# Key projection folded into the query projection, and expert indices from sixteen step positions

## The chip, the cores and the metric

The kernel runs on one core of a Trainium2 chip (TensorE, VectorE, ScalarE, POOL, and SyncE, which issues most transfers). The metric is the device time of one execution, in microseconds; the profile is of one further execution on the same kind of core.

## The reference

One encoder layer on 1024 tokens of width 1024, all in f32. A chunkwise mLSTM (4 heads of 256, chunks of 128 tokens, both directions) and an RG-LRU run side by side, are merged by sigmoid gates, and a product-key expert search follows. What the change touches:

```python
q = jnp.einsum("bshd,hde->bhse", xc, w_q)                  # xc = silu(conv(x))
k = jnp.einsum("bshd,hde->bhse", xc, w_k) / math.sqrt(d)   # q and k meet only as q . k
...
scores = jnp.einsum("thpc,hpnc->thpn", q, keys32)          # 8 heads, 2 halves, 128 keys
s_top, i_top = lax.top_k(scores, 16)
cand = s_top[:, :, 0, :, None] + s_top[:, :, 1, None, :]   # 16 x 16 sums
cand_idx = i_top[:, :, 0, :, None] * 128 + i_top[:, :, 1, None, :]
best, pos = lax.top_k(cand, 16)
idx = jnp.take_along_axis(cand_idx, pos, axis=-1)
gate = jax.nn.softmax(best, axis=-1)
act = gelu(expert_u[idx] . h)                              # 128 experts a token
out = sum_k (gate * act) * expert_v[idx]
```

The normalised scores are all that uses `k` in the mLSTM: within a chunk as q . k, between chunks through a state that sums k v and is read by q.

## The kernel before

Tiles have 128 partitions. Products that need precision are three products of rounded parts (`mm3`: high by high, high by low, low by high); others are plain f32 (`mm8`, `mm`).

Stages, in order. First the input projection with the LRU (to some 390 us). Then four mLSTM heads (some 400 to 920 us): `ml_x` projects and convolves a head's input, `ml_qkv` makes queries, keys and values, `ml_core` runs the chunks; merge-gate projections (`mg`) and output gates fill in. Working tiles come from one pool of 18 (`M1_BUFS`). `mixer_plan` lists the weights in order of use; an entry with an engine is split into high and low parts ahead of time, by ScalarE and POOL (`WENG`), an entry with None stays as loaded. Three raw weight buffers exist.

Then the branch merge in three groups of 2, 3 and 3 blocks of 128 tokens (L851, eight calls for each of 40 weight tiles a group), which ends in the scores of each block, kept in DRAM. Beside groups 1 and 2 runs `side`, a generator: for each of blocks 0 to 4 ("dense") `topk` finds the 16 best experts of each head and `gmat` turns indices and gates into a gate matrix over all 16384 experts; block 5 only gets `topk` (`prep`). The numbers that the generators yield are costs by which side work is laid beside the merge; the tile scheduler then fixes the order of each engine's queue ahead of the run.

`topk` takes the 16 best of 128 for the 16 half heads (`top16`), adds their scores along a staircase of 50 candidates that can be among the 16 best sums (`STAIR`: row a of the staircase has its own first position and length), and takes the 16 best of the 50 with their places. The indices of the winners come from a table `ci` of the 50 candidates' indices that POOL builds. For each head a one-hot matrix of 50 by 16 is made on VectorE (L1052), multiplied by the table on POOL (L1055) and reduced on VectorE (L1057). `gmat` splits each index by shift and mask (L1071 to L1075) into row and column, transposes them on TensorE and builds one-hot tiles (L1098, L1099, L1102; a quarter to a half of the L1102 products run on POOL).

The last stage (from some 1745 us) is the dense part: for each of 128 expert rows, products with all experts for five blocks (`ustep`, `vstep`), while the other three blocks fetch their own experts row by row (L1334, indirect transfers issued by POOL) into 8 row buffers, and VectorE multiplies and sums them (L1357, L1365). `topk` of blocks 6 and 7 is taken in steps between these, with the row buffers as its work tiles.

Of the kernel before, what the change touches and what calls it, by code (L numbers as in the profile page):

```python
# [8 lines left out]
F32 = mybir.dt.float32  # L9
F32R = mybir.dt.float32r  # L10
F16 = mybir.dt.float16
# [8 lines left out]
D = 1024  # L20
S = 1024
NB = 8
H = 4
# [11 lines left out]
class K:  # L35
# [13 lines left out]
    def x(self, dt=F32):  # L49
        return self.xp.tile([128, 1024], dt, name=self.name("x"), tag="x", bufs=self.x_bufs)  # L50
# [491 lines left out]
    def ml_x(self, h, done=None):  # L542

        nc = self.nc
        st = {}
        st["xm"], st["xc"] = [], []
        for e in range(2):
            blk = 2 * h + e
            x = self.pad_proj(blk, done if e == 0 else None)
            hi, lo = self.u(F32R), self.u(F32R)  # L550
            self.split(x[:, 2:2 + S], hi[:, :S], lo[:, :S])
            st["xm"].append((hi, lo))
            xc = self.u()
            self.conv(xc, x, V_MCW, V_MCB, blk)

            def act(xc=xc):
                nc.scalar.activation(xc[:, :S], xc[:, :S], AF.Silu)
                hi, lo = self.u(F32R), self.u(F32R)
                self.split(xc[:, :S], hi[:, :S], lo[:, :S])
                st["xc"].append((hi, lo))  # L560

            if e == 0:
                act()
            else:
                self.later = act
        return st

    def ml_qkv(self, h, st):
        nc = self.nc
        wh, wl = self.ws_get(("qk", h))  # L570
        for i, nm in enumerate(("q", "k")):
            st[nm] = []
            for e in range(2):
                t = self.u()
                for hf in range(2):
                    c = slice(hf * 512, hf * 512 + 512)
                    p = self.psg()
                    for cb in range(2):
                        o = i * 512 + cb * 256 + e * 128
                        self.mm3(p, (wh[:, o:o + 128], wl[:, o:o + 128]),  # L580
                                 (st["xc"][cb][0][:, c], st["xc"][cb][1][:, c]), cb == 0, cb == 1)
                    nc.scalar.activation(t[:, c], p, AF.Copy, scale=1.0 if i == 0 else 1.0 / 16.0)
                st[nm].append(t)
# [164 lines left out]
    def mixer_plan(self):  # L748
# [29 lines left out]
        for s_ in seq:  # L778
# [227 lines left out]
    def topk(self, b, res, x=None, keep=None):  # L1006
# [18 lines left out]
        ci = self.small([128, 8, self.NCAND], tag="ci", bufs=self.tb)  # L1025
        self.stair(nc.vector, cand, v)
        self.stair(nc.gpsimd, ci, ixf)
# [17 lines left out]
        idf = keep([128, 8, 16], tag="idf", bufs=2)  # L1045
        n = self.NCAND
        pr = [None] * 8
        for h in range(9):
            if h < 8:
                oh = self.small([128, n, 16], F16, tag="oh", bufs=2)  # L1050
                v8 = lambda z: z.rearrange("p a (u k) -> p a u k", k=8)
                nc.vector.tensor_tensor(v8(oh), self.iota_p[:, :, None, :].to_broadcast([128, n, 2, 8]),  # L1052
                                        v8(ph[:, h:h + 1].to_broadcast([128, n, 16])), op=OP.is_equal)
                pr[h] = x()[:, :n * 16].rearrange("p (a k) -> p a k", k=16)
                nc.gpsimd.tensor_tensor(pr[h], oh, ci[:, h][:, :, None].to_broadcast([128, n, 16]), op=OP.mult)  # L1055
            if h > 0:
                nc.vector.tensor_reduce(idf[:, h - 1], pr[h - 1].rearrange("p a k -> p k a"), axis=AX.X, op=OP.add)  # L1057
                pr[h - 1] = None
            if h % 2:
                yield 1.1  # L1060
        res["id"], res["gate"] = idf.rearrange("p h k -> p (h k)"), gate.rearrange("p h k -> p (h k)")
# [5 lines left out]
    def gmat(self, b, res):  # L1067

        nc = self.nc
        ii = self.x(I32)[:, 0:384].rearrange("p (a k) -> p a k", k=128)  # L1070
# [3 lines left out]
        ijf = self.x()[:, 0:256].rearrange("p (a k) -> p a k", k=128)  # L1074
        nc.vector.tensor_copy(ijf, ii[:, 1:3])  # L1075
        yield 1.0
# [232 lines left out]
    def prep(self, b, res, x=None):  # L1309
# [3 lines left out]
        self.nc.vector.tensor_copy(res["idi"], res["id"])  # L1313
        yield 0.1

    def gather(self, blocks):
        nc = self.nc
        KB = 8
        row = lambda: self.gkeep([128, D], tag="row", bufs=self.ROWS)
# [55 lines left out]
    def late_consts(self):  # L1375
        nc = self.nc
        A = self.A
        n = self.NCAND
        self.iota_p = self.cp.tile([128, n, 8], F16, name="iota_p")
        nc.gpsimd.iota(self.iota_p, pattern=[[1, n], [0, 8]], base=0, channel_multiplier=0, allow_small_or_imprecise_dtypes=True)  # L1380
# [171 lines left out]
def host(**i):  # L1552
# [10 lines left out]
    d["mwq"], d["mwk"], d["mwv"] = hw(a["mlstm_w_q"]), hw(a["mlstm_w_k"]), hw(a["mlstm_w_v"])  # L1563
# [30 lines left out]
```

## Time and profile before

| | |
|---|---|
| median of 3 runs | 3574.14 us (3561.7 to 3575.13) |
| profiled execution | 3566.02 us, span of its instructions 3563.9 us |
| TensorE / VectorE / ScalarE / POOL busy | 94% / 82% / 39% / 48% |

PE is TensorE's multiplying side and PEld its loading of weights, DVE is VectorE, ACT ScalarE. In a row of stretches the busy times stand in the order PE, PEld, DVE, ACT, POOL. A row of waits names the waiting engine, tile and line, and behind the arrow what it waited for. A group's last part is the idle time before its instructions. The share of the clock that TensorE was granted is 1.00 at its full 2.4 GHz.

### The profile page before, as it was taken

To read this page: it belongs to the slowest core of one execution; us is meant where nothing else is said; L and a number is where in the kernel's file an instruction comes from. 1 tells how busy PE (TensorE), PEld (TensorE's weight loads), DVE (VectorE), ACT (ScalarE), POOL (GpSimd) and SP (SyncE) were. 2 spreads that over 40 slices of the span, in tenths; PEclk is the share of its full clock that TensorE was granted. 3 is DMA by queue.
4 is the path that set the end of the run, shared out by engine and by line. 5 is a ranking of instruction groups with operands and counts; after the bars stand their busy time and mean duration, and the time that the engine had idled before them with its cause. 6 is when DMAs were issued, how large, how long until landed. Compare 5 with 4: busy or idle time off the path is not lost. (4 is left out here: it accounts for less than half of the span.)

```text
span 3563.9 us, 48538 instructions
## 1 busy us (share of the span) xinstructions
PE 3343.9 (94%) x17633; PEld 2827.0 (79%) x17633; DVE 2929.6 (82%) x5279; ACT 1392.0 (39%) x2565; POOL 1713.4 (48%) x1336
## 2 busy tenths in 40 slices
PE   7999999899899899878899999999999999999998
PEld 5787788778685565556788888998888999999987
DVE  8777574674327866998899999989999999999998
ACT  4565655655120240233333333343333334333333
POOL 7445354444102322342455555655555665666663
PEclk9999999999999999989899999999999999999999
DMA  2122211111466575558888879997887999999996
GB/s 107 60 71 68 72 51 51 63 48 44 154 217 208 159 251 199 174 170 258 312 318 301 283 275 342 360 338 276 314 284 279 341 357 351 344 347 334 352 348 239
DMA packets 319665, 812.56 MB, mean 228 GB/s; under 512 B 25600, under 2 KB 137408, under 8 KB 319424
## 3 DMA queue, kind: packets, MB, share of 16 engines
q0 software_dynamic: 115200, 419.48, 32.4%
q1 hardware_dynamic: 115184, 333.21, 26.7%
q10 hardware_dynamic: 89040, 56.76, 5.3%
q8 instruction: 138, 2.26, 0.3%
q14 instruction: 103, 0.84, 0.1%
HBM read 726.35 MB, written 83.00 MB: 227 GB/s over the span
## 5 line engine op out<-in xcount | busy, mean ns | idle before, releaser
L1334 POOL DMA_INDIRECT k<-in_pv,k x384 | 514.0, 1338 | 378.6 <-DVE k L1365 182.3
L1334 POOL DMA_INDIRECT k<-in_pu,k x384 | 506.6, 1319 | 332.7 <-DVE k L1357 148.0
L84 PE MATMUL ps<-h2h,wh 128*128 128x320 f32 x2048 | 637.2, 312 | 10.2 <-DVE u L1268 9.9
L85 PE MATMUL ps<-h2l,wh 128*128 128x320 f32 x2048 | 635.2, 310 | 0.0
L86 PE MATMUL ps<-h2h,wl 128*128 128x320 f32 x2048 | 628.9, 310 | 5.8 <-DVE wl L71 5.8
L851 PE MATMUL ps<-u,wr 128*128 128x384 f32 (+1 forms) x1920 | 581.1, 460 | 5.5 <-DMA u<-d 3.4
L1357 DVE SCALAR_TENSOR_TENSOR k<-k,rs,k 128x1024 f32<-128x1024 f32 x384 | 493.5, 1289 | 28.4 <-DMA k<-in_pu,k 28.4
L851 PEld LDWEIGHTS ps<-u,wr 128*128 128x128 f32 x1920 | 366.4, 194 | 181.7 <-issue 11.6
L85 PE MATMUL ps<-vl,wdh 128*128 128x512 f32 x1280 | 501.9, 393 | 2.5 <-DVE vl L71 2.5
L84 PE MATMUL ps<-vh,wdh 128*128 128x512 f32 x1280 | 469.0, 395 | 35.1 <-DVE u L1268 17.4
L1365 DVE SCALAR_TENSOR_TENSOR k<-k,k,k 128x1024 f32<-128x1024 f32 x384 | 494.6, 1288 | 0.4
L86 PE MATMUL ps<-vh,wdl 128*128 128x512 f32 x1280 | 494.3, 391 | 0.0
L84 PEld LDWEIGHTS ps<-h2h,wh 128*128 128x128 f32 x2048 | 388.1, 190 | 23.3 <-DVE u L1268 17.0
L86 PEld LDWEIGHTS ps<-h2h,wl 128*128 128x128 f32 x2048 | 385.6, 189 | 8.0 <-DVE wl L71 6.3
L85 PEld LDWEIGHTS ps<-h2l,wh 128*128 128x128 f32 x2048 | 387.8, 189 | 4.5
L1195 ACT ACTIVATE gel<-ps 128x320 f32<-128x320 f32 x256 | 111.1, 435 | 564.2 <-PE ps L86 549.4
L84 PEld LDWEIGHTS ps<-vh,wdh 128*128 128x128 f32 x1280 | 239.3, 189 | 88.2 <-DVE u L1268 22.5
L84 PE MATMUL ps<-h,wh 128*128 128x512 f32 x736 | 292.3, 399 | 14.0 <-ACT u L430 6.7
L86 PE MATMUL ps<-h,wl 128*128 128x512 f32 x736 | 290.8, 396 | 3.5 <-POOL wl L71 3.5
L85 PE MATMUL ps<-h,wh 128*128 128x512 f32 x736 | 291.0, 396 | 2.8 <-DVE h L253 2.8
L1238 ACT ACTIVATE gc<-gt 128x160 f32<-128x160 f32 x512 | 226.3, 510 | 155.9 <-DVE gel L1239 94.4
L86 PEld LDWEIGHTS ps<-vh,wdl 128*128 128x128 f32 x1280 | 241.4, 189 | 50.4
(327 smaller groups left out, 6079.1 us busy)
## 6 DMA issues: line engine op xcount, KB each, us to landing
wr<-in_u SPq DMA_DIRECT2D x128, 512.0 KB
wr<-in_v SPq DMA_DIRECT2D x128, 512.0 KB
d<-stg ACTq DMA_DIRECT2D x40, 1024.0 KB
gt<-d SPq DMA_DIRECT2D x64, 640.0 KB
wr<-in_win SPq DMA_DIRECT2D x49, 512.0 KB
wr<-in_wq SPq DMA_DIRECT2D x48, 512.0 KB
d<-u POOLq DMA_DIRECT2D x32, 512.0 KB
wr<-in_bm SPq DMA_DIRECT2D x24, 512.0 KB
```

The source lines that it names most:

```text
L84: mm(out, wh, mh, start=first, stop=False)
L85: mm(out, wh, ml, start=False, stop=False)
L86: self.lastmm = mm(out, wl, mh, start=False, stop=last)
L851: self.nc.tensor.matmul(p, w[:, cb * 128:cb * 128 + 128], m(cb), start=cb == 0, stop=cb == NB - 1)
L1195: nc.scalar.activation(gel[:, c], p, AF.Gelu)
L1238: nc.scalar.activation(gc[:, i * n:i * n + n], self.gt[j // 8, i][:, :, j % 8], AF.Copy)
L1334: nc.gpsimd.indirect_dma_start(out=t[:, :D], out_offset=None, in_=self.A["pu" if which == "u" else "pv"], in_offset=bass.IndirectOffsetOnA ...
L1357: nc.vector.scalar_tensor_tensor(r[:, :D], r[:, :D], self.rs2[:, b:b + 1], h2[:, :D], op0=OP.mult, op1=OP.mult, accum_out=dots[c][:, k % K ...
L1365: nc.vector.scalar_tensor_tensor(acc[:, :D], r[:, :D], ws[c][:, k % KB:k % KB + 1], acc[:, :D], op0=OP.mult, op1=OP.add)
```

## The change

The weights of queries and keys are handed over transposed and are no longer split. At the start of `ml_qkv` their product over the head's inner dimension is formed on TensorE in plain f32, scaled, and split in two parts; queries are projected with it, and the raw convolved input takes the keys' place in `ml_core`.

In `topk` the row of a winner in the staircase is the number of row starts that its place has reached. So its first index is the first of the list plus the sum of the steps between neighbours of the sorted list up to that row. Places of all 8 heads (128 numbers a token) are compared at once with 16 starts (`past`), multiplied by the steps (`steps`) and summed over 16 by halving (`total`). The start of the row is found in the same way and subtracted, and what is left selects the second index. All runs on VectorE, in 16-bit floats, over 16 x 128 elements. Row and column come out apart, so `gmat` takes them as they are; `prep` joins them again for the fetches.

```diff
@@ ml_x
+                st["k"].append(xc)
@@ ml_qkv
-        wh, wl = self.ws_get(("qk", h))
-        for i, nm in enumerate(("q", "k")):
...
+        raw = self.ws_get(("qk", h))
+        p = self.psg()
+        for cb in range(2):
+            for eb in range(2):
+                nc.tensor.matmul(p[:, cb * 256:cb * 256 + 256], raw[:, eb * 256 + cb * 128:eb * 256 + cb * 128 + 128],
+                                 raw[:, 512 + eb * 256:512 + eb * 256 + 256], start=eb == 0, stop=eb == 1)
+        t = self.u(F32R)
+        wh, wl = t[:, 0:512], t[:, 512:1024]
+        nc.scalar.activation(wh, p, AF.Copy, scale=1.0 / 16.0)
+        nc.vector.scalar_tensor_tensor(wl, p, 1.0 / 16.0, wh.bitcast(F32), op0=OP.mult, op1=OP.subtract)
+        st["q"] = []
...
@@ mixer_plan
-                plan.append((("qk", h), [(self.A["mwq"][h], 512), (self.A["mwk"][h], 512)], 1024, WENG))
+                plan.append((("qk", h), [(self.A["mwq"][h], 512), (self.A["mwk"][h], 512)], 1024, None))
@@ topk
-        ixf = self.small([128, 8, 2, 16], tag="tif", bufs=self.tb)
-        nc.vector.tensor_copy(ixf, ix)
-        nc.vector.tensor_scalar(ixf[:, :, 0], ixf[:, :, 0], 128.0, None, op0=OP.mult)
+        ixh = self.small([128, 2, 17, 8], F16, tag="ixh", bufs=self.tb)
+        nc.gpsimd.memset(ixh[:, :, 0], 0.0)
+        nc.vector.tensor_copy(ixh[:, :, 1:17], ix.rearrange("p h i a -> p i a h"))
+        dix = self.small([128, 2, 128, 2], F16, tag="dix", bufs=self.tb)
+        for i in range(2):
+            up, dn = (ixh[:, i, o:o + 16].rearrange("p a h -> p (a h)")[:, :, None].to_broadcast([128, 128, 2]) for o in (1, 0))
+            nc.vector.tensor_tensor(dix[:, i], up, dn, op=OP.subtract)
-        self.stair(nc.gpsimd, ci, ixf)
...
-        for h in range(9):
-            if h < 8:
-                oh = self.small([128, n, 16], F16, tag="oh", bufs=2)
...
-                nc.gpsimd.tensor_tensor(pr[h], oh, ci[:, h][:, :, None].to_broadcast([128, n, 16]), op=OP.mult)
-            if h > 0:
-                nc.vector.tensor_reduce(idf[:, h - 1], pr[h - 1].rearrange("p a k -> p k a"), axis=AX.X, op=OP.add)
...
+        def past(o, x, i):
+            nc.vector.tensor_tensor(octs(o), octs(x[:, None, :].to_broadcast([128, 16, 128])), tab(i), op=OP.is_ge)
+
+        def steps(o, m, i):
+            nc.vector.tensor_tensor(o.rearrange("p a (h u t) -> p (a h) u t", u=8, t=2),
+                                    m.rearrange("p a (h u t) -> p (a h) u t", u=8, t=2),
+                                    dix[:, i, :, None, :].to_broadcast([128, 128, 8, 2]), op=OP.mult)
+
+        def total(o, z):
+            for n in (8, 4, 2):
+                nc.vector.tensor_tensor(z[:, 0:n], z[:, 0:n], z[:, n:2 * n], op=OP.add)
+            nc.vector.tensor_tensor(o, z[:, 0], z[:, 1], op=OP.add)
+
+        m, z = wide(x(F16)), wide(x(F16))
+        past(m, pos, 0)
+        steps(z, m, 0)
+        total(ij[:, 0], z)
+        yield 3.6
+        nc.vector.tensor_tensor(octs(z), octs(m), tab(1), op=OP.mult)
+        rest = self.small([128, 2, 128], F16, tag="rest", bufs=self.tb)
+        total(rest[:, 0], z)
+        nc.vector.tensor_tensor(rest[:, 1], pos, rest[:, 0], op=OP.subtract)
+        yield 2.6
+        past(m, rest[:, 1], 2)
+        steps(z, m, 1)
+        total(ij[:, 1], z)
+        yield 3.6
@@ gmat
-        nc.vector.tensor_copy(ii[:, 0], res["id"])
-        nc.vector.tensor_single_scalar(ii[:, 1], ii[:, 0], 7, op=OP.logical_shift_right)
-        nc.vector.tensor_single_scalar(ii[:, 2], ii[:, 0], 127, op=OP.bitwise_and)
...
-        nc.vector.tensor_copy(ijf, ii[:, 1:3])
-        yield 1.0
+        ijf = res["ij"]
@@ prep
-        self.nc.vector.tensor_copy(res["idi"], res["id"])
+        self.nc.vector.scalar_tensor_tensor(res["idi"], res["ij"][:, 0], 128.0, res["ij"][:, 1], op0=OP.mult, op1=OP.add)
@@ late_consts
+        self.ranks = self.cp.tile([128, 3, 16, 8], F16, name="ranks")
...
+        for a in range(16):
+            nc.gpsimd.memset(self.ranks[:, 0, a], float(first[a]))
+            nc.gpsimd.memset(self.ranks[:, 1, a], float(first[a] - first[max(a - 1, 0)]))
```

## Rows read from the trace of the kernel before

**Rows 1.** The page's totals: busy time (share of the span) and instructions.

```profile
PE 3343.9 (94%) x17633; PEld 2827.0 (79%) x17633; DVE 2929.6 (82%) x5279; ACT 1392.0 (39%) x2565; POOL 1713.4 (48%) x1336
```

**Rows 2.** Stretches: length, busy us (instructions) by engine, granted clock, DMA share, GB/s.

```profile
400.00:830.00 430.00, 403.67 (x2146) 345.71 (x2146) 261.27 (x572) 251.34 (x603) 196.94 (x216) 0.95 0.18 56
1100.00:1340.00 240.00, 218.97 (x1146) 142.49 (x1145) 199.90 (x526) 63.40 (x121) 76.53 (x54) 0.96 0.64 202
1340.00:1660.00 320.00, 285.03 (x1395) 184.28 (x1394) 277.69 (x854) 73.22 (x135) 97.15 (x70) 0.94 0.59 188
1660.00:1750.00 90.00, 60.58 (x426) 55.52 (x425) 75.07 (x208) 31.86 (x60) 36.15 (x30) 0.81 0.88 303
1900.00:2740.00 840.00, 808.27 (x4467) 730.07 (x4466) 791.17 (x1232) 307.81 (x542) 487.78 (x363) 0.99 0.85 304
2740.00:3540.00 800.00, 795.46 (x4438) 722.25 (x4437) 759.03 (x955) 304.69 (x542) 487.02 (x369) 1.00 0.93 342
```

**Rows 3.** Waits of TensorE, 1090 to 1870 us: total, times, longest.

```profile
PE pg L1116 <- DVE g L1098: 26.7, 10, 4.4
```

**Rows 4.** TensorE's timeline: start us, us, instruction; first and last of thirteen, then f32.

```profile
418.22 0.40 PE L84 MATMUL pg<-u,wh 128*128 128x512 f32 x1
...
421.02 0.39 PE L84 MATMUL pg<-u,wh 128*128 128x512 f32 x1
...
974.69 2.97 PE L851 MATMUL ps<-u,wr 128*128 128x256 f32 x13
```

**Rows 5.** TensorE's groups by shape, the merge's with 256 columns.

```profile
L851 PE MATMUL ps<-u,wr 128*128 128x256 f32 x640 | 142.2, 383 | 4.2 <-DMA u<-d 3.4 <-DMA wr<-in_bm 0.8
```

**Rows 6.** VectorE's groups by shape: line, instruction, count, busy us, mean ns, idle before.

```profile
L1357 DVE SCALAR_TENSOR_TENSOR k<-k,rs,k 128x1024 f32<-128x1024 f32 x384 | 493.5, 1289 | 28.4 <-DMA k<-in_pu,k 28.4
...
L1098 DVE TENSOR_TENSOR g<-iota_n,g 128x1024 f16<-128x1024 f16 x80 | 88.2, 1104 | 1.1 <-PE pg L1117 1.0
...
L1057 DVE TENSOR_REDUCE s<-x 128x16 f32<-128x800 f32 x40 | 59.9, 1499 | 0.3 <-POOL x L1055 0.3
...
L1052 DVE TENSOR_TENSOR s<-iota_p,s 128x800 f16<-128x800 f16 x64 | 39.1, 621 | 0.1
...
L731 DVE SCALAR_TENSOR_TENSOR u<-pg,c,u 128x512 f32<-128x512 f32 x16 | 11.1, 744 | 0.6 <-PE pg L729 0.5
...
L1072 DVE TENSOR_SCALAR x<-x 128x128 int32<-128x128 int32 x5 | 2.7, 539 | 0.1
...
L1022 DVE CAST s<-s 128x256 f32<-128x256 uint32 x8 | 2.3, 293 | 0.0
```

**Rows 7.** Single lines on VectorE: count, duration ns minimum/median/maximum, first and last start.

```profile
L1052 DVE TENSOR_TENSOR s<-iota_p,s x64: 552/568/2106, 1105.8 to 2695.8; 128x800 f16<-128x800 f16 x64
...
L1098 DVE TENSOR_TENSOR g<-iota_n,g x80: 665/685/2384, 1127.0 to 1694.3; 128x1024 f16<-128x1024 f16 x80
...
L1043 DVE TENSOR_TENSOR k<-k,s x3: 293/1093/1641, 1710.1 to 2647.9; 128x128 f32<-128x128 f32 x3
```

**Rows 8.** POOL's groups by shape.

```profile
L1102 POOL TENSOR_TENSOR g<-g,g 128x1024 f16<-128x1024 f16 x40 | 86.4, 2160 | 241.1 <-PE pg L1117 99.7 <-DVE g L1085 56.4 <-PE ps L851 21.3
L1055 POOL TENSOR_TENSOR x<-s,s 128x800 f32<-128x800 f16 x48 | 81.3, 1699 | 90.6 <-DVE s L1052 71.7 <-issue 18.2 <-DMA wr<-in_bl 0.7
```

**Rows 9.** The timeline near 1219 us, VectorE beside POOL.

```profile
1219.25 2.34 POOL L1102 TENSOR_TENSOR g<-g,g 128x1024 f16<-128x1024 f16 x1
1219.76 2.38 DVE L1098 TENSOR_TENSOR g<-iota_n,g 128x1024 f16<-128x1024 f16 x1
```

**Rows 10.** The same view in stretches of 100 us.

```profile
1100.00:1200.00 100.00, 88.33 (x419) 55.01 (x418) 99.13 (x355) 12.17 (x24) 35.24 (x31) 0.97 0.56 181
...
1400.00:1500.00 100.00, 86.54 (x418) 54.39 (x419) 99.36 (x299) 14.93 (x29) 31.28 (x22) 0.93 0.56 176
```

**Rows 11.** Waits of all engines, 1900 to 2740 us.

```profile
PE ps L84 <- DVE u L1268: 26.4, 19, 3.7
...
DVE k L1357 <- DMA k<-in_pu,k: 20.6, 18, 4.4
```

More of the change, by code (lines that the diff above doesn't have):

```diff
@@ L49, in x @@
     def x(self, dt=F32):
-        return self.xp.tile([128, 1024], dt, name=self.name("x"), tag="x", bufs=self.x_bufs)
+        return self.xp.tile([128, 2048 if dt == F16 else 1024], dt, name=self.name("x"), tag="x", bufs=self.x_bufs)
     def ps(self):
@@ L545, in ml_x @@
         st = {}
-        st["xm"], st["xc"] = [], []
+        st["xm"], st["xc"], st["k"] = [], [], []
         for e in range(2):
@@ L569, in ml_qkv @@
         nc = self.nc
-        wh, wl = self.ws_get(("qk", h))
-        for i, nm in enumerate(("q", "k")):
[L572 to L583, printed above, removed]
+        raw = self.ws_get(("qk", h))
[9 more added lines that the diff above has]
+        st["q"] = []
+        for e in range(2):
+            t = self.u()
+            for hf in range(2):
+                c = slice(hf * 512, hf * 512 + 512)
+                p = self.psg()
+                for cb in range(2):
+                    o = cb * 256 + e * 128
+                    self.mm3(p, (wh[:, o:o + 128], wl[:, o:o + 128]),
+                             (st["xc"][cb][0][:, c], st["xc"][cb][1][:, c]), cb == 0, cb == 1)
+                nc.scalar.activation(t[:, c], p, AF.Copy)
+            st["q"].append(t)
         wh, wl = self.ws_get(("v", h))
@@ L1061, in topk @@
-        res["id"], res["gate"] = idf.rearrange("p h k -> p (h k)"), gate.rearrange("p h k -> p (h k)")
+        ij = keep([128, 2, 128], tag="ij", bufs=2)
+        pos = ph.rearrange("p h k -> p (h k)")
+        wide = lambda z: z[:, 0:2048].rearrange("p (a k) -> p a k", k=128)
+        octs = lambda z: z.rearrange("p a (u k) -> p a u k", k=8)
+        tab = lambda i: self.ranks[:, i, :, None, :].to_broadcast([128, 16, 16, 8])
+        def past(o, x, i):
+            nc.vector.tensor_tensor(octs(o), octs(x[:, None, :].to_broadcast([128, 16, 128])), tab(i), op=OP.is_ge)
@@ L1064, in gsmall @@
+        res["ij"], res["gate"] = ij, gate.rearrange("p h k -> p (h k)")
     def gsmall(self, shape, dt=F32, tag="s", bufs=2):
@@ L1069, in gmat @@
         nc = self.nc
-        ii = self.x(I32)[:, 0:384].rearrange("p (a k) -> p a k", k=128)
-        nc.vector.tensor_copy(ii[:, 0], res["id"])
-        nc.vector.tensor_single_scalar(ii[:, 1], ii[:, 0], 7, op=OP.logical_shift_right)
-        nc.vector.tensor_single_scalar(ii[:, 2], ii[:, 0], 127, op=OP.bitwise_and)
-        ijf = self.x()[:, 0:256].rearrange("p (a k) -> p a k", k=128)
-        nc.vector.tensor_copy(ijf, ii[:, 1:3])
-        yield 1.0
+        ijf = res["ij"]
         p = self.psg()
@@ L1318, in gather @@
         KB = 8
-        row = lambda: self.gkeep([128, D], tag="row", bufs=self.ROWS)
+        row = lambda dt=F32: self.gkeep([128, 2 * D if dt == F16 else D], dt, tag="row", bufs=self.ROWS)
         nxt = self.first
@@ L1377, in late_consts @@
         A = self.A
-        n = self.NCAND
-        self.iota_p = self.cp.tile([128, n, 8], F16, name="iota_p")
-        nc.gpsimd.iota(self.iota_p, pattern=[[1, n], [0, 8]], base=0, channel_multiplier=0, allow_small_or_imprecise_dtypes=True)
+        self.ranks = self.cp.tile([128, 3, 16, 8], F16, name="ranks")
+        first = [o + i * nb for a, na, nb, o in self.STAIR for i in range(na)]
+        for a in range(16):
+            nc.gpsimd.memset(self.ranks[:, 0, a], float(first[a]))
+            nc.gpsimd.memset(self.ranks[:, 1, a], float(first[a] - first[max(a - 1, 0)]))
+        nc.gpsimd.iota(self.ranks[:, 2], pattern=[[1, 16], [0, 8]], base=0, channel_multiplier=0, allow_small_or_imprecise_dtypes=True)
         self.iota_n = self.gp.tile([128, 128, 2], F16, name="iota_n")
@@ L1562, in host @@
     hw = lambda m: f(m[0].reshape(H, 2, 128, 256).transpose(0, 2, 1, 3).reshape(H, 128, 512))
-    d["mwq"], d["mwk"], d["mwv"] = hw(a["mlstm_w_q"]), hw(a["mlstm_w_k"]), hw(a["mlstm_w_v"])
+    ht = lambda m: hw(m.reshape(1, H, 256, 256).transpose(0, 1, 3, 2))
+    d["mwq"], d["mwk"], d["mwv"] = ht(a["mlstm_w_q"]), ht(a["mlstm_w_k"]), hw(a["mlstm_w_v"])
     lw = lambda m: f(m[0].transpose(1, 2, 0, 3).reshape(8, 128, 256))
```

11 lines of the change are left out of this document (removed).

## The prediction

> **What bounds the kernel now.** I read the page's totals first, then the busy time of every engine in stretches, then the waits of TensorE, and last the durations of single lines. The totals name no winner: TensorE is busy for 94% of the span, VectorE for 82% [rows 1]. The stretches do, and the reader should take the idle part of each in turn [rows 2]. From 400 to 830 us (the four mLSTM heads) TensorE has work for 404 of 430 us and VectorE for 261: TensorE bounds. From 1100 to 1660 us the product-key search and the gate matrices run beside the branch merge. There TensorE stands for 21 us of 240 and for 35 of 320, and it waits first of all for VectorE's one-hot tiles [rows 3]. From 1660 to 1750 us, where merge is over, it stands for 29 of 90 us. In the dense phase it stands for 32 of 840 us while two more searches run on VectorE (1900 to 2740), and for only 5 of 800 once they are over. So VectorE costs time only where a search runs; elsewhere TensorE's own work counts. The granted clock tells the same: 0.94 to 0.96 of full in the two search stretches, 1.00 once TensorE no longer stands; what that may give back I leave to the range.
>
> **The change, part by part.**
>
> *Keys folded into queries (4 heads).* Each head drops two blocks by two halves by two row blocks by three products, 24 matmuls of 512 columns. Their busy figure of 0.40 us is not their price, since they are pipelined: thirteen starts, 418.22 to 421.02, are 2.80 us apart, so 0.233 us each [rows 4], 5.6 us a head. Added are four unsplit f32 products of 256 columns. Such a product stands as two records in the trace (the 320 calls of the merge group with 256 columns leave 640 records [rows 5]); thirteen records take 2.97 us, or (2.97 - 0.38) / 12 = 0.216 us each [rows 4, 5], so 8 x 0.216 = 1.7 us. Net 3.9 us a head, 15.5 us in all.
> The new product must be evicted (a ScalarE copy, then a VectorE pass like the one over 512 PSUM columns, 0.74 us [rows 6]) before the queries can start. I cost that at nothing: it needs only weights, and the value and merge-gate projections that TensorE mixes into this stretch can run meanwhile. Without that cover it is about twice 0.74, 1.5 us a head, 6 us. ScalarE loses four evictions and one split a head, POOL one subtraction; neither bounds here. The raw conv output now lives until the core has transposed it: up to two more of the 18 working tiles from the x projections on, two fewer new ones at the queries. For the tightest place, the first head behind the LRU, and for the eviction together I subtract 3 us. I take 12 us; the ends are 15.5 and, with 6 us for the chain and some 2.4 us at each head, 0.
>
> *Index search (8 blocks), on VectorE.* Removed per block: eight compares and eight reductions, 8 x (0.62 + 1.50) = 17.0 us [rows 6], and the cast and multiply of indices, 0.3 us and less, together 0.5 us. A dense block also drops four conversions in the gate matrix: 0.54 us, another cast of 256 and two smaller ones, 1.3 us [rows 6]. A 128-column multiply takes 1.09 us in the middle and 0.29 at the least [rows 7]; the long ones stand beside POOL's products, so 0.8 us more. Old sum: 19.5 us.
> The new operations do not stand in the trace. The nearest are 16-bit tensor operations with the same patterns (runs of 8, and pairs): 0.568 us for 800 elements, 0.685 for 1024 [rows 7]. A line through the two gives 0.15 us plus 0.52 ns an element: 1.22 us for 2048, 0.68, 0.42 and 0.28 for the halvings, and 0.22 to 0.28 for 128. Five passes over 2048 are 6.1 us, three folding sums 4.9, two differences with a repeated element 0.8 (between the 0.29 of a 256 cast [rows 6] and twice that; I take 0.4 each), the cast 0.35, the small difference 0.2: 12.4 us. A dense block thus gains 7.1 us, a gathered one, which had no conversions but gets a slightly dearer last step, 5.8. The other bound is one element a cycle: the 1024-column f32 row of 1.29 us [rows 6] makes a pass 2.3 us and the sum some 21 us, 1.5 us worse than now.
>
> *POOL's part.* Eight products of 1.7 us and a seven-piece table a block go [rows 8]; a memset of 16 columns comes. A VectorE operation that starts beside a POOL product is drawn out to POOL's end: a compare at 1219.76 takes 2.38 us beside a product of 2.34 us from 1219.25 [rows 9]. The compares of this line average 1.10 us against a median of 0.685 [rows 6, 7], 33.5 us over 80, and two more lines do the same. Most of that belongs to the gate matrices' own POOL products, which stay. I put 20 us over the five dense blocks on the products that go, an estimate (0 to 35).
>
> *What of it reaches the end.* First stretch: two blocks, 14 + 8 us cut, 21 us idle; VectorE is saturated for about half of it [rows 10]: 10 us. Second: three blocks, 21 + 12 us cut, 35 us idle, and VectorE has 278 of 320 us [rows 2, 10]: 18. Next late there is TensorE's own merge work, so not all. Tail: block 5's search stands alone in front of the gather, 5.8 us cut: 5. Dense phase: 11.6 us cut from two searches, some more since gather products on VectorE are no longer drawn out, and row fetches no longer queue behind POOL products; TensorE has 32 us idle, of it 26 behind a VectorE addition, and VectorE waits 21 us for rows [rows 11]: 10 (0 to 20). The two 16-bit work tiles take two of the eight row buffers, as the two product tiles did.
>
> Sum: 12 + 10 + 18 + 5 + 10 = 55 us. The profiled execution took 3566.02 us, 8 us under the median of the runs but inside them; 3566 - 55 = 3511 us.
>
> **The rivals.**
> *VectorE's gain stays hidden.* TensorE's queue is a fixed order; if its own matmuls fill the stretches anyway, or the 16-bit passes run at one element a cycle, only the projection counts: 3566 - 12 = 3554 us. For it: TensorE is 89 to 91% busy there [rows 2]. Against: its waits name VectorE tiles [rows 3].
> *All of it arrives.* 15.5 + 21 + 33 + 6 + 17 = 92 us, 3474 us. For it: VectorE is full for whole hundreds of us there [rows 10]. Against: the merge cannot shrink below TensorE's work.
> *The tile pool starves.* The longer-lived conv output delays the next head by some 5 us at each of four heads: the 12 us become minus 8, and the time 3531 us. No tile wait stands among TensorE's waits now, but the pool is nearly full.
> *Slower: POOL holds the new passes up.* Twenty 16-bit operations a block now stand on VectorE, and the gate matrix of the block before runs eight POOL products of 2.2 us beside them [rows 8]. If each waited half such a product, 1.1 us, a block would lose 22 us and gain 11; five blocks end 55 us worse, and with the 12 and 10 us of the other parts the time is 3566 + 55 - 22 = 3599 us. It decides from a mean delay of 0.55 us on, where the search gains nothing. Rows against it: the compare line now mixed with POOL averages 0.42 us over its median, the search's own only 0.05 [rows 6, 7].
> The Trainium skill (SBUF — State Buffer, Who interferes with whom) has a rule for this rival: a VectorE instruction with two SBUF inputs contends with a GpSimd instruction that reads SBUF, and the one that starts second fully blocks. By that rule alone every pass that meets a product waits for its rest, and the sum would be nearer to 3599 us the more often they meet; the trace agrees with the blocking (2.38 beside 2.34 us), and by its means the meetings are too rare.
>
> **How the numbers follow.** Half a per cent, 18 us, is about what a measurement of this kernel tells from no change: faster means under 3556 us, slower over 3592. Forecast (3490 to 3535) 0.54; all of it 0.14; starved pool 0.09; hidden 0.17, of which half lands within 0.5%; slower rival 0.06, of which 0.05 beyond 0.5%. Faster: 0.54 + 0.14 + 0.09 + 0.08 = 0.85, less 0.04 for an order that comes out worse in places I can't see, 0.81; same 0.13; slower 0.06. The range leaves out the slower rival, half of the hidden case beyond 3556 us and the far end of the best one: 3474 to 3556 us.
>
> **What would show it.** Right: the heads' stretch ends some 12 us earlier with VectorE's load there unchanged; the new 2048-element passes take 1.2 us; the 128-column multiply falls to 0.3 us; POOL has no 800-column products; TensorE's idle time between 1100 and 1750 us falls from 85 to some 50 us, and in 1900 to 2740 from 32 to about 20. Wrong: passes of 2 us and more, either by rate (all of them) or by POOL (some of them); a stand of TensorE in front of the queries for the folded weights; or unchanged idle time between 1100 and 1750 us although VectorE's busy time fell, which would mean that the fixed order of TensorE's queue, and not VectorE's load, made it.

## The result and the profile after

Four runs of the changed kernel take 3482.6 us (median; 3478.55 to 3484.26), beside 3574.64 us (3561.7 to 3577.22) for the kernel before: ratio 0.9748, interval 0.9723 to 0.9773. Profiled execution against profiled execution it is 3484.26 us against 3566.02 us, 81.8 us less; forecast were 55. The direction was right, and so was what bounds each stage; the size lies near the rival "all of it arrives" (3474 us), though not by its parts, as the account further down shows.

First the page's totals, to be read against [rows 1]:

```profile
PE 3303.4 (95%) x17569; PEld 2806.3 (81%) x17569; DVE 2852.5 (82%) x5287; ACT 1384.3 (40%) x2550; POOL 1574.0 (45%) x1252
```

The shares say little again. I cut both spans at two places which do not depend on the order of side work: the first matmul of the merge, and the first product that the dense stage shares over all experts (its `vstep`). A table of their starts in the two traces, in us:

| | before | after | gain | forecast |
|---|---|---|---|---|
| up to the merge | 923.2 | 902.1 | 21.1 | 12 |
| merge and what follows it | 819.6 | 781.3 | 38.3 | 10 + 18 + 5 |
| dense stage, to the end of the span | 1821.0 | 1799.1 | 21.9 | 10 |

Next the stretches of before up to the merge, then merge groups 1 and 2 (columns as in [rows 2]):

```profile
395.00:923.20 528.20, 484.52 (x2608) 416.23 (x2608) 322.91 (x739) 303.98 (x745) 236.02 (x267) 0.95 0.16 53
1076.30:1356.30 280.00, 258.97 (x1285) 167.16 (x1285) 213.19 (x613) 67.51 (x128) 76.78 (x54) 0.97 0.64 205
1356.30:1660.10 303.80, 268.83 (x1331) 173.69 (x1330) 277.79 (x854) 71.63 (x132) 97.15 (x70) 0.94 0.59 187
```

and the same three of after:

```profile
395.00:902.10 507.10, 468.83 (x2537) 405.49 (x2537) 327.58 (x741) 294.20 (x729) 224.98 (x263) 0.93 0.17 54
1058.10:1319.50 261.40, 253.31 (x1287) 164.70 (x1286) 196.74 (x611) 68.06 (x128) 46.00 (x26) 1.00 0.68 220
1319.50:1599.70 280.20, 260.39 (x1306) 168.35 (x1305) 241.37 (x847) 67.98 (x127) 55.58 (x28) 0.98 0.63 201
```

Up to the merge TensorE is busy for 15.7 us less and idle for 5.4 us less (43.7 to 38.3). In group 1 it is idle for 8.1 us instead of 21.0, in group 2 for 19.8 instead of 35.0: 28.1 us together, the 10 + 18 of the forecast. (Idle time is the length of a stretch less PE's busy time.) But the groups became 18.6 and 23.6 us shorter, 42.2 in all. The other 14.1 us is TensorE's busy time, 5.7 and 8.4 us less for the same work: the granted clock rose from 0.97 and 0.94 to 1.00 and 0.98, and busy time times clock stays at 251 to 255 us in all four rows.

In the first row the clock moved the other way, from 0.95 to 0.93, although TensorE stood less. Busy time times clock falls there from 460 to 436 us, by 24 us and not by 15.7: by the rounded clocks, the lower one cost some 10 us (an estimate). Why it fell, no run here shows.

What TensorE still waits for between 1030 and 1800 us; the one-hot line L1123 (L1098 before) takes 15.9 us where it took 26.7 in [rows 3]:

```profile
PE ps L84 <- ACT wdh L78: 17.5, 1, 17.5
PE pg L1141 <- DVE g L1123: 15.9, 11, 3.8
PE pg L1141 <- ACT stg L1144: 10.6, 4, 4.6
PE pg L1141 <- DVE g L1127: 6.4, 5, 2.3
```

VectorE's groups by shape (`past` L1066, `steps` L1069, the second sum's product L1083, the halvings L1075, differences L1038 and L1086, the 128-column multiply L1056 that was L1043), against [rows 6, 7]:

```profile
L1123 DVE TENSOR_TENSOR g<-iota_n,g 128x1024 f16<-128x1024 f16 x80 | 72.8, 910 | 1.5 <-PE pg L1142 1.4
L1066 DVE TENSOR_TENSOR x<-s,ranks 128x2048 f16<-128x2048 f16 x12 | 14.6, 1218 | 0.3
L1069 DVE TENSOR_TENSOR x<-x,s 128x2048 f16<-128x2048 f16 x12 | 14.6, 1216 | 0.0
L1075 DVE TENSOR_TENSOR x<-x 128x1024 f16<-128x1024 f16 x18 | 13.5, 748 | 0.1
L1075 DVE TENSOR_TENSOR x<-x 128x512 f16<-128x512 f16 x18 | 10.6, 590 | 0.2
...
L1038 DVE TENSOR_TENSOR s<-s 128x256 f16<-128x256 f16 x16 | 6.0, 413 | 0.0
...
L1086 DVE TENSOR_TENSOR s<-s,s 128x128 f16<-128x128 f16 x8 | 3.3, 412 | 0.1
...
L1056 DVE TENSOR_TENSOR s<-s,s 128x128 f32<-128x128 f32 x5 | 1.4, 281 | 0.0
```

A pass over 2048 elements takes 1.218 us (1.22 forecast) and the multiply 0.28 us (0.29). The folded product, in TensorE's timeline, stands 5 us ahead of the queries that need it: that of the second head begins at 539.20 us, its eight records end 1.89 us later, other projections go on behind it, and the first product of the queries starts at 546.15 us.

```profile
539.20 1.89 PE L576 MATMUL pg<-wr 128*128 128x256 f32 x8
540.73 0.58 PE L85 MATMUL ps<-h,wh 128*128 128x512 f32 x1
...
546.15 0.40 PE L84 MATMUL pg<-u,u 128*128 128x512 f32 x1
```

Last the dense stage, from its first shared product to the last and from there to the end, before:

```profile
1742.90:3553.10 1810.20, 1771.24 (x9792) 1601.31 (x9792) 1712.33 (x2490) 681.89 (x1211) 1056.81 (x790) 0.99 0.88 321
3553.10:3563.80 10.70, 0.02 (x1) 0.00 (x0) 5.82 (x11) 2.69 (x7) 0.00 (x0) 0.62 0.48 196
```

and after:

```profile
1683.40:3473.20 1789.80, 1761.76 (x9792) 1600.41 (x9792) 1684.98 (x2495) 681.88 (x1212) 1013.06 (x761) 0.99 0.89 324
3473.20:3482.40 9.20, 0.00 (x0) 0.00 (x0) 4.42 (x9) 1.76 (x6) 0.00 (x0) 0.64 0.47 194
```

VectorE has 28.8 us less to do there (1718.2 to 1689.4), and the stage gets 21.9 us shorter. On TensorE's side 10.9 us of that are idle time over the shared products (39.0 to 28.0), 9.5 us are busy time for the same 9792 records, and 1.5 us are the end behind them. Within the stage 19.2 us come from the first 9/16 of the shared products, in which the two searches run (1042.5 to 1023.3 us from the stage's first product); the rest takes 767.4 and 766.1 us.

### The profile page after: what moved, and what is told of

It is laid out like the page before. It is cut to its first block, busy times and chain, and to the rows that moved or that the text cites. A ratio compares the mean times of both kernels' runs of the same rounds, so it can differ in the third digit from the quotient of the medians.

```text
span 3482.5 us, 48268 instructions
## 1 busy us (share of the span) xinstructions
PE 3303.4 (95%) x17569; PEld 2806.3 (81%) x17569; DVE 2852.5 (82%) x5287; ACT 1384.3 (40%) x2550; POOL 1574.0 (45%) x1252
## 4 chain that ended last, share of the span: by engine, by line
PE 60%; DVE 21%; DMA 8%; issue 6%; ACT 3%; POOL 1%; SPq 0%; ACTq 0%; DVEq 0%; POOLq 0%
PE ps L84 15%; PE ps L85 15%; PE ps L86 15%; PE ps L861 9%; DMA wr<-in_u 3%; DMA k<-in_pu,k 2%; DVE k L1382 2%; DVE k L1390 2%; POOL k L1359 1%; PE pg L84 1%; PE pg L85 1%; PE pg L86 1%; DVE g L1127 1%; DVE u L1293 1%; DVE vl L71 1%
## 5 line engine op out<-in xcount | busy, mean ns | idle before, releaser
L84 PE MATMUL ps<-h2h,wh 128*128 128x320 f32 x2048 | 637.4, 312 | 13.6 <-DVE u L1293 11.1
L861 PE MATMUL ps<-u,wr 128*128 128x384 f32 (+1 forms) x1920 | 571.6, 455 | 10.6 <-DMA u<-d 8.8
L84 PEld LDWEIGHTS ps<-h2h,wh 128*128 128x128 f32 x2048 | 386.9, 189 | 25.9 <-DVE u L1293 15.5
L85 PEld LDWEIGHTS ps<-vl,wdh 128*128 128x128 f32 x1280 | 241.6, 189 | 50.1 <-DVE vl L71 3.8
## 6 DMA issues: line engine op xcount, KB each, us to landing
gt<-d SPq DMA_DIRECT2D x64, 640.0 KB, 10.9
```

The lines of the kernel that those rows point to most:

```text
L84: mm(out, wh, mh, start=first, stop=False)
L85: mm(out, wh, ml, start=False, stop=False)
L861: self.nc.tensor.matmul(p, w[:, cb * 128:cb * 128 + 128], m(cb), start=cb == 0, stop=cb == NB - 1)
```

## The experiments

The theory was that each half acts for itself: TensorE's own work falls by the projections, and VectorE's load in the search stretches and the dense stage sets how long TensorE stands. The rivals were POOL's products (they draw out VectorE's passes, and their absence is the gain) and the order of the queues. The three stages of every run, cut as above (us, from the profiled execution), with the medians and the ratios to the kernel before on the same chip:

| run | to merge | merge | dense | median | ratio, interval |
|---|---|---|---|---|---|
| before | 923.2 | 819.6 | 1821.0 | | |
| after | 902.1 | 781.3 | 1799.1 | 3482.6 | 0.9748 [0.9723, 0.9773] |
| e11_after_again | 901.7 | 780.0 | 1796.9 | 3482.97 | 0.9761 [0.9743, 0.9778] |
| e1_fold_only | 902.4 | 810.2 | 1819.5 | 3534.59 | 0.9909 [0.9893, 0.9926] |
| e2_index_only | 920.5 | 785.1 | 1795.7 | 3505.15 | 0.9824 [0.9807, 0.984] |
| e3_vector_load | 902.8 | 796.6 | 1814.7 | 3513.55 | 0.9844 [0.9827, 0.986] |
| e4_pool_back | 903.0 | 830.5 | 1810.5 | 3549.86 | 0.9951 [0.9935, 0.9968] |
| e5_pool_write | 902.3 | 796.6 | 1803.7 | 3502.03 | 0.981 [0.9793, 0.9826] |
| e6_lo_vector | 902.7 | 758.3 | 1789.3 | 3455.02 | 0.9686 [0.967, 0.9702] |
| e7_gather_old | 899.8 | 780.9 | 1821.2 | 3507.4 | 0.983 [0.9813, 0.9846] |
| e8_fold_split | 907.3 | 783.4 | 1805.1 | 3500.47 | 0.9818 [0.9802, 0.9834] |
| e9_gather_old_vector | 902.1 | 791.9 | 1830.0 | 3526.71 | 0.9875 [0.9857, 0.9892] |
| e10_before_lo_vector | 920.8 | 785.8 | 1821.8 | 3533.14 | 0.99 [0.9882, 0.9917] |
| e12_reduce_load | 903.0 | 805.9 | 1817.1 | 3530.87 | 0.9892 [0.9871, 0.9912] |

**Each half alone.** e1 has the folded projection and the old search; e2 the new search and the old projection.

```diff
@@ e1: before, and of the change only
-        wh, wl = self.ws_get(("qk", h))
+        raw = self.ws_get(("qk", h))
...
@@ e2: after, and in ml_qkv and mixer_plan the lines of before
-        raw = self.ws_get(("qk", h))
+        wh, wl = self.ws_get(("qk", h))
```

> Only the key projection is folded into the queries'; the index search is the old one. Theory (TensorE's time in the four heads is what the fold saves, 3.9 us net a head, and it arrives whole): 15 to 22 us faster than before, 3553 to 3560 us, the merge starting that much earlier and everything behind it unchanged. Rival (the fold matters only together with a lighter VectorE): under 8 us. Rival (the fold also moves later stages): over 30 us.

> Only the index search is the new one; query and key projections are the old ones. Theory (the two parts act in different stages and add up): 60 to 77 us faster than before, 3498 to 3515 us; with the fold alone it makes up the 92 us of both. Rival (the parts overlap): the two single gains sum to over 110 us or under 75 us.

Measured: e1 33 us less than before by the medians (the forecast gave this half 12), e2 62 us less. Together 95, and the whole change gives 87 to 92: the halves nearly add. By the profiled executions of the table they make 94.6 us and the whole 81.8, and most of the difference lies in the two later stages. e2 came out inside its range. e1 missed its own, and its rival "also moves later stages" is the one that came: 20.8 us fall up to the merge, and 9.4 more behind the merge's start, where the code is that of before. All of these lie between the merge's last matmul and the first shared product (73.2 us instead of 82.8); I take them for a different order of the queues.

**The weights split as before.** e8 takes the weights of queries and keys split by ScalarE and POOL again and forms the folded product from the parts.

```diff
@@ e8: after
-                nc.tensor.matmul(p[...], raw[...], raw[...], start=eb == 0, stop=eb == 1)
+                self.mm3(p[:, cb * 256:cb * 256 + 256], (wh[:, a], wl[:, a]), (wh[:, m], wl[:, m]), eb == 0, eb == 1)
...
-                plan.append((("qk", h), [...], 1024, None))
+                plan.append((("qk", h), [...], 1024, WENG))
```

> The changed kernel with the weights of queries and keys split ahead on ScalarE and POOL as before, and the folded weights made of three products of their parts (1.4 us of TensorE a head instead of 1.7). Theory (the heads gained 21 us: 15 to 18 from TensorE's work, the rest from the split and the evictions that left ScalarE and POOL): the merge begins 2 to 5 us later than in the changed kernel, at 904 to 907 us. Rival (the split was idle cover and counts for nothing): it begins at 900 to 902 us.

The merge begins at 907.3 us, 5.2 us later, at the far end of the theory's range. TensorE's waits up to the merge have one that is not in after:

```profile
PE ps L84 <- ACT wh L78: 6.4, 1, 6.4
```

TensorE waits there for a ScalarE copy of another weight. So the split that the change drops was worth some 5 us; the forecast had it at nothing, since no engine that does it bounds. The dense stage got 6 us longer too, with code that is the same: order again, not explained.

**VectorE's load put back.** e3 repeats the first and the last comparing pass three times more each, 7.3 us of VectorE in a block. e12 does as much with five strided reductions like the old ones (of the comparison tile, as sums, where the text below says maxima); nothing reads them.

```diff
@@ e3: after
-        past(m, pos, 0)
+        for _ in range(4):
+            past(m, pos, 0)
...
-        past(m, rest[:, 1], 2)
+        for _ in range(4):
+            past(m, rest[:, 1], 2)
@@ e12: after
+        def sums(n):
+            for _ in range(n):
+                s_ = self.small([128, 16], tag="sums", bufs=2)
+                nc.vector.tensor_reduce(s_, mt[:, 0:1600].bitcast(F32).rearrange("p (a k) -> p k a", k=16), axis=AX.X, op=OP.add)
...
+        sums(3)
...
+        sums(2)
```

> The changed kernel with six extra compare passes over 2048 elements a block, 6 x 1.22 = 7.3 us of VectorE work, so that VectorE's search load is back at the old 19.5 us while POOL stays free of it; the result is the same. Theory (VectorE's load is the larger part of the search's gain, POOL's share a quarter): 30 to 50 us slower than the changed kernel, 3513 to 3533 us. Rival (the freed POOL port is the larger part): at most 15 us slower, under 3498 us.

> The kernel after, with five reductions more in each dense block: maxima over groups of 50 of the 800 numbers of a comparison tile, read with the stride of the old search's reductions, three behind the first comparing pass and two behind the last; nothing reads what they give. At the old reductions' price of about 1.5 us each they put some 7.5 us of VectorE into a block, as the six passes of the vector-load run did (7.3 us), in the other form. Theory: it is the form of the old search, its slow strided reductions, that makes TensorE stand in the last stage; then the last stage (first to last shared v product) takes 1800 us or more and the total 3520 us or more. Rival: the last stage absorbs any VectorE work of that size there, whatever its form, as in the vector-load run; then it takes 1783 to 1796 us and the total is 3505 to 3522 us. If the rival holds, what is left of the 20 us that the last stage gained is the order of the queues, and stays open.

e3 comes out inside its range, 31 us above the kernel after; e12 48 us. e12's reductions cost what the old ones did:

```profile
L1084 DVE TENSOR_REDUCE s<-x 128x16 f32<-128x800 f32 x30 | 44.0, 1501 | 0.1
...
L1084 DVE TENSOR_REDUCE s<-k 128x16 f32<-128x800 f32 x10 | 15.1, 1551 | 0.0
```

The two put the same time on VectorE, and e12 is 12 us slower by the profiled executions, 17 by the medians; whether that is the form, the place or the order of the queues, no run separates.

Where it is paid, the stretches of e3 show: merge groups 1 and 2, then from the merge's last matmul to the first shared product.

```profile
1060.80:1322.80 262.00, 255.02 (x1286) 165.00 (x1285) 207.26 (x623) 67.34 (x128) 48.87 (x26) 0.99 0.70 219
1322.80:1595.30 272.50, 256.85 (x1259) 164.72 (x1258) 244.46 (x846) 66.34 (x122) 48.54 (x25) 0.97 0.64 201
1595.30:1699.40 104.10, 59.66 (x474) 55.63 (x472) 89.97 (x235) 35.05 (x58) 26.72 (x17) 0.73 0.80 266
```

The two groups are 7 us shorter than in after, and TensorE stands in them for 22.6 us, not for the 56.0 of before. Only 13.6 us more of VectorE's work lie there; the rest moved behind the merge, where the last stretch takes 104.1 us instead of 83.7 and VectorE has 90.0 us to do instead of 68.5. In e12 the groups are 9.6 us longer, with 34.7 us of idle time, and the last stretch 16.6. So the two runs show that VectorE's added time is paid, most of it behind the merge; that the old search's load on VectorE alone made TensorE stand in the groups, they do not show.

e12's total lies where the theory had it and its stretch of shared products where the rival had it: neither text looked past the last product. The end of the dense stage, e3:

```profile
1699.40:3487.60 1788.20, 1762.38 (x9792) 1601.39 (x9792) 1688.16 (x2492) 674.65 (x1198) 1025.08 (x760) 0.99 0.90 323
3487.60:3514.00 26.40, 0.00 (x0) 0.00 (x0) 14.75 (x24) 8.84 (x19) 0.00 (x0) 0.55 0.29 119
```

and e12:

```profile
1709.00:3501.60 1792.60, 1761.63 (x9792) 1599.12 (x9792) 1690.22 (x2492) 676.13 (x1198) 1010.58 (x760) 0.99 0.90 322
3501.60:3526.00 24.40, 0.04 (x1) 0.00 (x0) 12.71 (x22) 8.84 (x19) 0.00 (x0) 0.55 0.31 129
```

The shared products take no longer than in after, but 26.4 and 24.4 us remain behind them instead of 9.2: the gathers, whose last multiplication (the scaling of their last block) ends 9.5 us before TensorE's last product in after (3463.7 and 3473.2 us), now end 11.0 and 8.9 us behind it. VectorE has 13.5 us more to do in the stage in both runs (1702.9 against 1689.4), and the stage is 15.6 and 18.0 us longer. Here it is paid in full.

**The old search in the gathered blocks.** e7 runs the old search in blocks 5, 6 and 7 only; e9 does that and takes its table and its products from POOL to VectorE.

```diff
@@ e7: after, topk of the gathered blocks
+        old = b not in self.slot
+        if old:
...
+            self.stair(nc.gpsimd, ci, ixf)
...
+                    nc.gpsimd.tensor_tensor(pr[h], oh, ci[:, h][:, :, None].to_broadcast([128, n, 16]), op=OP.mult)
@@ e9: e7, and
-            self.stair(nc.gpsimd, ci, ixf)
+            self.stair(nc.vector, ci, ixf)
...
-                    nc.gpsimd.tensor_tensor(pr[h], oh, ...
+                    nc.vector.tensor_tensor(pr[h], oh, ...
```

> The changed kernel with the old index search in the three blocks that fetch their experts (5, 6 and 7); the dense blocks keep the new one. Theory (the dense phase gained 21 us because POOL's products left the searches that run inside it): the first product of the last stage stands where the changed kernel has it or up to 6 us later, the stage itself is 15 to 24 us longer, 3498 to 3512 us in all. Rival (the stage gained by the order of its start, not by its own searches): within 8 us of the changed kernel.

> The old index search in the blocks that fetch (5, 6 and 7), as in the run of that name, but with its table and its eight products made on VectorE: POOL is out of the search, VectorE has some 8 us a block more than in the old one and 13 us more than in the new one. Theory (the dense phase lost its 21 us to POOL's products, not to VectorE's load): the last stage takes 1785 to 1798 us from its first product of the second kind to the last, against 1790 in the changed kernel and 1812 with products on POOL. Rival (VectorE's load in the searches counts): 1808 us or more. Rival (the order of queues that comes with the old search): 1808 us or more as well, with no VectorE pass drawn out.

e7 gives back 22.1 us in the dense stage and nothing ahead of it: that stage's gain is the new search in two blocks, as put. Its rows:

```profile
1680.70:3493.00 1812.30, 1770.38 (x9792) 1600.49 (x9792) 1717.72 (x2491) 682.21 (x1214) 1051.48 (x790) 0.99 0.89 321
3493.00:3501.80 8.80, 0.04 (x1) 0.00 (x0) 4.00 (x8) 1.44 (x4) 0.00 (x0) 0.80 0.45 183
```

VectorE's 32 us more (1721.7) are paid by standing shared products here, not by late gathers. In e9 the shared products take 1807.2 us:

```profile
1694.00:3501.20 1807.20, 1767.83 (x9792) 1600.87 (x9792) 1706.50 (x2510) 674.03 (x1199) 1026.01 (x765) 0.99 0.89 321
```

That is 9 us above the theory's range and just short of the 1808 us of both rivals, and the stage as a whole is 30.9 us longer than in after. My theory for e9 fell: the stage is as long without POOL's products, when VectorE has nearly as much to do (1717.6 us). That does not clear the products in e7. There some 18 of the 32 us are VectorE passes that they drew out (by the count given under "POOL's share"), and in e9 VectorE's own products take their place.

Over all fourteen profiled executions the stage is 99 to 123 us longer than VectorE's busy time in it. That spread is as wide as the effects of e3 and e12: at VectorE's 1689 to 1690 us the stage takes 1789.3 (e6) to 1805.1 us (e8). So it follows VectorE's time, but at what rate, these runs do not settle.

**POOL's reads.** e4 adds eight products of 768 elements on POOL to each block; nothing reads them. e5 adds sixteen fills of the same size to each block, eight at each of the two places, which read nothing.

```diff
@@ e4: after, ahead of the first pass and behind the difference, four products each
+                d_ = self.small([128, 6, 128], tag="spin", bufs=1)
+                s_ = a[:, None, :].to_broadcast([128, 6, 128])
+                nc.gpsimd.tensor_tensor(d_, s_, s_, op=OP.mult)
@@ e5: after, at the same places, eight each, behind a copy of 8 elements on VectorE
+                nc.gpsimd.memset(d_, 0.0)
```

> The changed kernel with eight POOL products of 768 elements a block put back, four when the places are known and four at the last compare; nobody reads them, so only POOL's time and its port count. Theory (POOL's share is a quarter of the search's gain): 10 to 25 us slower than the changed kernel, 3493 to 3508 us, the 16-bit passes on VectorE being drawn out beside them. Rival (the port is the larger part): over 35 us slower. Rival (POOL costs nothing): within 4 us.

> The run before, but POOL's extra work in each block only writes: each four products over 768 elements become eight memsets of 768, tied to the same places by a copy of eight elements on VectorE. Theory (a product on POOL costs because it reads SBUF while VectorE reads two inputs; POOL's own time does not count): within 8 us of the changed kernel, under 3490 us, and no VectorE pass drawn out beside a memset. Rival (POOL's queue is what counts, because fetches and gate products wait in it): 25 us or more slower than the changed kernel, over 3505 us.

e4 costs 67 us over after, far out of its range and in that of its rival "over 35 us". In merge groups 1 and 2 TensorE stands for 56.4 us again, as in before (56.0), and the clock falls to 0.96 and 0.95:

```profile
1057.70:1339.50 281.80, 260.84 (x1287) 168.55 (x1286) 214.58 (x611) 68.46 (x128) 80.42 (x42) 0.96 0.65 204
1339.50:1640.30 300.80, 265.41 (x1307) 170.81 (x1306) 263.75 (x847) 67.82 (x127) 99.39 (x52) 0.95 0.60 187
```

VectorE is busy there for 40 us more than in after, with no operation more: its passes are drawn out. The timeline, POOL beside VectorE:

```profile
1156.82 4.32 POOL L1082 TENSOR_TENSOR s<-s 128x768 f32<-128x768 f16 x2
1157.33 2.48 DVE L1069 TENSOR_TENSOR x<-x,s 128x2048 f16<-128x2048 f16 x1
```

A pass of 1.21 us takes 2.48 us beside a product, as the compare did in [rows 9]; 12 of the `steps` passes had a median of 2.29 us. In e5's timeline the same pass beside eight fills in a row takes 1.20 us:

```profile
1107.11 6.31 POOL L1082 MEMSET s<- 128x768 f32 x8 [12.82 <-DVE s L1080]
1108.63 1.20 DVE L1069 TENSOR_TENSOR x<-x,s 128x2048 f16<-128x2048 f16 x1
```

So it is POOL's reading that holds this pass up, not its being busy. The Trainium skill (SBUF — State Buffer, Who interferes with whom) has both halves: an instruction of VectorE with two SBUF inputs contends with a GpSimd instruction that reads SBUF, not with one that only writes it. The traces agree. This also bears on why the old search's own products did less harm than e4's (some 40 us of VectorE passes drawn out against some 80, by the count under "POOL's share"): for 40 of the 115 us that they took, a reduction ran beside them, which has one input. In before, by line, none of the reductions is drawn out, while POOL's products take 1.59 us in the median beside the merge, 2.07 in the dense stage, and up to 2.95:

```profile
L1057 DVE TENSOR_REDUCE s<-x x40: 1474/1498/1530, 1108.3 to 1586.3; 128x16 f32<-128x800 f32 x40
L1057 DVE TENSOR_REDUCE k<-k x16: 1477/1528/1584, 2030.7 to 2710.2; 128x16 f32<-128x800 f32 x16
...
L1055 POOL TENSOR_TENSOR x<-s,s x48: 1546/1591/2471, 1106.5 to 1724.7; 128x800 f32<-128x800 f16 x48
...
L1055 POOL TENSOR_TENSOR k<-s,s x16: 1547/2070/2953, 2024.7 to 2702.1; 128x800 f32<-128x800 f16 x16
```

e5 still lost 20 us, more than its theory's 8 and less than its rival's 25, most of it behind the merge's first matmul (15.3). The fills stand in POOL's queue ahead of its gate-matrix products; that this is what the 20 us are, I did not show.

**The products that stay.** e6 gives VectorE the 40 low-part products of the gate matrices that POOL had in after; e10 does it to the kernel before.

```diff
@@ e6: after; e10: before
-LO_LAST = (0, 2)
+LO_LAST = ()
...
-LO_POOL = (0, 2)
+LO_POOL = ()
```

> The changed kernel with the 40 products of the gate matrices that POOL does (8 a dense block, 2.3 us each) given to VectorE as well (0.68 us each). Theory (they hold VectorE up for some 50 us in all, and VectorE would take 27 us for them): VectorE is relieved by some 20 us, 5 to 15 us faster than the changed kernel, 3468 to 3478 us. Rival (VectorE's own load alone counts): 8 us or more slower.

> The kernel before with the 40 gate-matrix products of POOL given to VectorE; the index search stays the old one, its products on POOL. Theory (POOL's reads beside two-input passes of VectorE cost more than the load they take off it, in the old kernel too): 12 to 28 us faster than before, 3541 to 3557 us. Rival (the move pays only where the search is light on VectorE): within 8 us of before, or slower.

> The changed kernel once more, on the chip of the two runs beside it: 3473 to 3487 us.

Both gain more than expected: 28 us over after run again on the same chip, 37 us over before. e6 is the best kernel of this study, 3455.02 us, and beats both. VectorE by shape, first after and then e6 (L1127 is that line; its 40 products on POOL took 2296 ns each in after):

```profile
L1127 DVE TENSOR_TENSOR g<-g,g 128x1024 f16<-128x1024 f16 x120 | 101.0, 854 | 24.8 <-PE pg L1141 24.7
...
L1127 DVE TENSOR_TENSOR g<-g,g 128x1024 f16<-128x1024 f16 x160 | 112.0, 716 | 46.9 <-PE pg L1141 46.6
L1123 DVE TENSOR_TENSOR g<-iota_n,g 128x1024 f16<-128x1024 f16 x80 | 57.5, 718 | 3.3 <-PE pg L1142 3.1
```

and its merge groups 1 and 2:

```profile
1056.30:1312.90 256.60, 253.20 (x1286) 164.72 (x1285) 181.22 (x627) 67.90 (x128) 10.91 (x10) 1.00 0.71 224
1312.90:1583.10 270.20, 261.19 (x1354) 169.38 (x1354) 235.56 (x878) 72.18 (x134) 10.47 (x9) 0.98 0.68 214
```

VectorE does 40 operations more and is busy for 15.5 and 5.8 us less than in after, since the means fall: L1123 from 0.91 to 0.72 us, L1127 from 0.85 to 0.72. TensorE stands there for 12.4 us instead of 27.9. The dense stage is 9.8 us shorter too, with the same code and the same load on VectorE: order again, not explained. e11, the kernel after again, repeats its total and its stages within 3 us.

## Why the prediction was right, and where it was small

- **Right: what bounds.** TensorE's own work up to the merge, VectorE's time from there. e1 and e2 show the halves to be nearly separate. Over all fourteen profiled executions TensorE's idle time in merge groups 1 and 2 goes with VectorE's busy time in them: 12.4 us at 416.8 (e6), 22.6 to 37.2 at 436 to 463, 49.6 to 56.4 at 478 to 491. How much of VectorE's time is its own load and how much is passes drawn out by POOL stays open: of the 62 us of the search alone (e2), 7.3 to 7.5 us of load put back into each block take 31 and 48.
- **Right: the prices.** Passes 1.218 us for 1.22, multiply 0.28 for 0.29, f32 records 0.216 apart. The block's search sums to some 13.4 us for 12.4: five passes 6.1, three sums 5.7 (4.9 forecast; some halvings are drawn out), differences 0.8 and 0.4, the cast 0.4. (The 0.4 of the small difference is a mean of eight with one of 1.8 us beside a POOL product; the median is 0.22, the 0.2 forecast.)
- **Too small: the fold, 12 for 21.1.** TensorE's busy time fell by 15.7 us where 15.5 were forecast, but that agreement is partly luck, since the clock of the stretch fell as well and hid some of the work that left. The 3 us that I took off for the eviction and the tile pool did not come: the product is formed ahead of its use. And the dropped split, costed at nothing, is worth 5 us (e8).
- **Too small: the search beside the merge, 28 for 42.** The idle time of TensorE fell by just the 28 us; the step that fell short is that the clock was left to the range: at 1.00 and 0.98 instead of 0.97 and 0.94 the same work took 14.1 us less. e4 shows the way back: with its idle time the clock of groups 1 and 2 falls to 0.96 and 0.95. The 5 us of the tail did not show: from the merge's last matmul to the first shared product it takes 82.8 us before and 83.7 after. With 2.9 us lost in group 0 (153.1 to 156.0), which no step had, the stage gains 38.3 us.
- **Too small: the dense stage, 10 for 21.9.** I priced it by TensorE's idle time there, 26 us behind a VectorE addition, and halved. That idle time fell as forecast, by 10.9 us over the shared products. What the price left out is again busy time for the same work, 9.5 us; the rows' clock, 0.99 in both, is too coarse to say whether the clock gave it back. And there is a second chain, the gathers on VectorE, that ends 5 us ahead of TensorE's last product in before (3547.9 and 3553.1 us): VectorE's time comes out as standing products (e7) or as late gathers (e3, e12).
- **POOL's share, 20 us for the dense blocks: about right beside the merge, and missing in the dense stage.** Counting in the trace of before what VectorE's two-input passes took beyond their shape's tenth percentile while a product of L1055 ran, I get 23 to 27 us beside the merge, by how the shapes are grouped, and 16 in the dense stage, half of it the gathers' own multiplications, which the forecast named and gave no size.
- **Rivals.** "Hidden" and "starved pool" did not come. "All of it arrives" came near in the time and not in the way: of its 21 and 33 us beside the merge 18.6 and 23.6 came, a third of them by the clock, and of its 6 us in the tail nothing. The slower one did not, since products and passes seldom meet: in after, products of L1127 cost three halvings 4.4 us in all. e4 shows that it would: eight products a block are enough to take back most of the gain.

Open: the 9.4 us of e1 behind the merge's start and the 6 us of e8 and 9.8 us of e6 in the dense stage, where the code was not touched; I take them for the order of the queues, which no run tested. Any single effect of 10 us in this account could be such a shift; the two halves (33 and 62 us) are well above it.

## What to carry to other kernels

A stage in which TensorE looks nearly full can have a second chain that ends with it; compare the end of both before you take TensorE's idle time as the price, and look past its last product. Where VectorE makes TensorE stand, removing the stand can give back the idle time and then the clock, as it did beside the merge and not in the heads' stretch; take both from the rows. And before an operation is given to POOL to unload VectorE, count what its reads add to VectorE's two-input passes: 40 products of 2.3 us on POOL cost more than 40 of 0.7 us on VectorE.

## What the runs showed of the hardware

That POOL's fills (0.74 us each) leave VectorE's passes at 1.20 us where its products make them 2.48 was known as a rule, not in these numbers. That a strided reduction of 800 elements takes 1.5 us and was not drawn out in any of 56 (at most 1.58 us), I had not looked at before e4. And I had not expected that VectorE's busy time could fall by 31 us (2852.5 to 2821.4 over the span) when it is given 40 operations more.
